# The FFN's hidden units: 128x128 transposes on TensorE through PSUM, or 32x32 block transposes on VectorE

## The chip, the core and the metric

The kernel runs on one core of one Trainium2 chip. The metric is the time of one execution on the device, in microseconds (us), as the median of several runs. The core's engines run side by side: TensorE (PE in the profile, with its weight loads as PEld), VectorE (DVE), ScalarE (ACT), GpSimd (POOL) and SyncE (SP), which here issues the loads of the weights.

## What is computed

The reference is one layer of a decoder trunk for 256 tokens of width 2048. First comes a token mixer, which the change doesn't touch, then a feed-forward network (FFN) with 5632 inner units:

```python
def channel_mixing(h, w_gate_up, w_down, g_pre, g_post):
    xn = rmsnorm(h, g_pre)
    gu = jnp.einsum('bld,df->blf', xn, w_gate_up)
    gate, up = gu[..., :FFN_HIDDEN], gu[..., FFN_HIDDEN:]
    y = jnp.einsum('blf,fd->bld', jax.nn.silu(gate) * up, w_down)
    return rmsnorm(y, g_post)
```

All of it is float32. The kernel keeps the precision by splitting each operand into a rounded part `hi` and a remainder `lo`, and by three matmuls for each product (hi·hi, hi·lo, lo·hi).

## The kernel before

**Splitting weights.** `load` (L84 to L88) brings 1 MB of weights into one of three `raw` buffers by a DMA from SP's queue. `split` (L90 to L98) makes two pairs `hi`, `lo` of 128x1024 elements from it: ScalarE casts `raw` into `hi` (L95), VectorE subtracts `hi` from `raw` into `lo` (L96). There are four `hi` and four `lo` buffers. So a cast waits until TensorE is through with the buffer four pairs earlier, the subtraction waits for the cast, TensorE waits for both, and the next load of a `raw` buffer waits for its last subtraction.

**Gate and up.** The loop over `gi` (L829) goes through 11 groups of 512 inner units. In each, `c` runs over four blocks of 512 input features and `s` over gate and up; for each of these 1 MB is loaded and split into two pairs (`gu_load`), and `gu_part` issues the matmuls L738, L739, L740: the stationary side is the normed input `x2hi` or `x2lo` (128 features x 128 tokens), the moving side 512 columns of weights. A pair takes 12 matmuls (two k, two token halves i, three products), a group 192. For c below 3 the pairs are used one after the other; for c = 3 each token half i is finished in turn, and `gu_evac` (L742) then takes the two banks out of PSUM: ScalarE's Silu writes `hg` (L745), VectorE multiplies by the up half (L746). `hg` has tokens on its partitions and 512 units in its rows, one tile for each half i, with four buffers in the pool `ft`. Even groups accumulate in the four PSUM banks `mx`, odd groups in the four `acc`.

**Turning.** The down product needs the units on the partitions. `hidden_out(gi, hgs, bank)` (L751) does that one group late, behind block c = 0 of the next group, so that TensorE doesn't wait for `hg`: for each half i, four TensorE transposes of 128x128 (L764, with `ident`) into a PSUM bank, then ScalarE's cast into `hidhi` (L767, 128x512) and VectorE's subtraction into `hidlo` (L768, 128x512). The last group's call stands in the down product, behind its first chunk (`after_first`, L646). Groups 0 to 3 of the units lie in tiles that reuse the mixer's place (`hid`), groups 4 to 10 in two tiles of the pool `hp` (`hid2`).

**Down.** `ktile_product` (L623) runs over the output's two halves and over 44 blocks k of 128 units, two k for each load of 1 MB and one `hi`, `lo` pair for each k. Here the hidden units are the stationary side and the weights the moving one: 12 matmuls for each k (two i, two j, three products; L628, L629, L630).

**Order.** The program is written in one order, and a scheduler of the framework puts each engine's instructions in a fixed sequence: of those whose inputs are there in its own model of the time, the one that stands first in the program goes first. Each engine then works through its sequence strictly in order, waiting on semaphores.

Of the kernel before, what the change touches and what calls it, by code (L numbers as in the profile page):

```python
# [10 lines left out]
F32 = mybir.dt.float32  # L11
F32R = mybir.dt.float32r
BF16 = mybir.dt.bfloat16
AF = mybir.ActivationFunctionType
ALU = mybir.AluOpType
# [3 lines left out]
P = 128  # L19
# [3 lines left out]
NT = 256  # L23
T = NMETA + NT
HID = 5632
NF = HID // P
# [11 lines left out]
def tile_hybrid_layer(  # L38
# [20 lines left out]
    vec, act, pe, pool, sp = nc.vector, nc.scalar, nc.tensor, nc.gpsimd, nc.sync  # L59
# [12 lines left out]
    def nm(s):  # L72
        uid[0] += 1
        return f"{s}_{uid[0]}"

    def acc(i):
        return psa.tile([P, 512], F32, tag=f"acc{i}", name=nm("acc"))

    def mx():
        return psm.tile([P, 512], F32, tag="mx", name=nm("mx"))  # L80
# [3 lines left out]
    def load(view, nk, w):  # L84
        raw = rawp.tile([P, 2 * MB], F32, tag="raw", name=nm("raw"), bufs=RAWB)
        r = raw[:, : nk * w].rearrange("p (k c) -> p k c", c=w)
        sp.dma_start(out=r, in_=view)
        return r  # L88
# [16 lines left out]
    ident = cst.tile([P, P], F32, name="ident")  # L105
# [29 lines left out]
    def win_view(k0, nk, c0, w):  # L135
        return w_in[0, k0 * P : (k0 + nk) * P, c0 : c0 + w].rearrange("(k p) c -> p k c", p=P)
# [402 lines left out]
    def first(kind, i):  # L539

        if kind in ("sbq", "o"):
            return NMETA
        if kind == "q":
            return NMETA - 4
        if kind == "pool":
            return NMETA - WINDOWS[i]
        return 0

    def load_group(ka, kb, blocks):
        nb = len(blocks)  # L550
        starts = [base[kind] + P * i for kind, i in blocks]
        raw = rawp.tile([P, 2 * MB], F32, tag="raw", name=nm("raw"), bufs=RAWB)
        r = raw[:, : (kb - ka) * nb * P].rearrange("p (k c) -> p k c", c=nb * P)
        j = 0
        while j < nb:
            e = j + 1
            while e < nb and starts[e] == starts[e - 1] + P:
                e += 1
            sp.dma_start(out=r[:, :, j * P : e * P], in_=win_view(ka, kb - ka, starts[j], (e - j) * P))
            j = e  # L560
        return r

    for gi, blocks in enumerate(groups):
        nb = len(blocks)
        w = P * nb
        accs = [acc(b) for b in range(nb)]
# [5 lines left out]
        for ka, kb in spans:  # L572
            if gi == 0:
# [5 lines left out]
                r = chunks[ka] if ka in chunks else load(win_view(ka, kb - ka, OG, 396), kb - ka, 396)  # L579
            else:  # L580
                r = load_group(ka, kb, blocks)
            subs = []
            for k0 in range(ka, kb, 2):
                rs = r[:, k0 - ka : k0 - ka + 2]
                if gi == 0:
                    gsrc = rs[:, :, 0:12].rearrange("p k (a b) -> p k a b", a=2)
                    dst = [gw[:, j, k0 : k0 + 2, :].rearrange("p k (a b) -> p k a b", a=2)[:, :, :, 0:6]
                           for j in range(2)]
                    for a in range(2):
                        act.copy(out=dst[0][:, :, a], in_=gsrc[:, :, a])  # L590
                        vec.tensor_tensor(out=dst[1][:, :, a], in0=gsrc[:, :, a], in1=dst[0][:, :, a].bitcast(F32),
                                          op=ALU.subtract)
                    rs = rs[:, :, 12:]
                subs.append((k0, split(rs, 2, w)))
            last = kb == KT
            passes = [subs] if last else [[s] for s in subs]
            for ss in passes:
                for b, (kind, i) in enumerate(blocks):
                    ts = slice(first(kind, i), T)
# [20 lines left out]

    mhi, mlo_ = mix_tiles()

    def ktile_product(wview, nk, half, accs, lhs, on_block, ticks=False, before_tail=None, after_first=None):  # L623

        def three(k, i, j, h, l):
            lh, ll = lhs(k, i)
            o, js = accs[i][j], slice(j * 512, (j + 1) * 512)
            pe.matmul(o, lhsT=lh, rhs=h[:, 0, js], start=k == 0, stop=False)  # L628
            pe.matmul(o, lhsT=lh, rhs=l[:, 0, js], start=False, stop=False)  # L629
            pe.matmul(o, lhsT=ll, rhs=h[:, 0, js], start=False, stop=k == nk - 1)  # L630

        pend = []
        for ci in range(0, nk, 2):
            r = load(wview(ci, half), 2, 1024)
            for kk in range(2):
                pend.append((ci + kk, split(r[:, kk : kk + 1], 1, 1024)))
            if ci + 4 < nk:
                for k, (h, l) in pend:
                    for i in range(2):
                        for j in range(2):  # L640
                            three(k, i, j, h, l)
                        if ticks:
                            tick()
                pend = []
            if ci == 0 and after_first:
                after_first()  # L646
        if before_tail:
            before_tail()
        for i in range(2):
            for j in range(2):  # L650
                for k, (h, l) in pend:
                    three(k, i, j, h, l)
                on_block(i, j)
# [36 lines left out]
    assert not queue and not active and not quick  # L690
    mixst.close()
    fp = ctx.enter_context(tc.tile_pool(name="fp", bufs=1))
    ft = ctx.enter_context(tc.tile_pool(name="ft", bufs=4, side="right"))
    exst = ExitStack()
    yp = exst.enter_context(tc.tile_pool(name="yp", bufs=1))
    ex = exst.enter_context(tc.tile_pool(name="ex", bufs=4))
# [42 lines left out]
                pe.matmul(o, lhsT=x2hi[:, k, ts], rhs=l[:, kk, :], start=False, stop=False)  # L739
                pe.matmul(o, lhsT=x2lo[:, k, ts], rhs=h[:, kk, :], start=False, stop=k == KT - 1)  # L740

    def gu_evac(banks, i):  # L742
        sc = rr[:, 1, i : i + 1]
        hg = ft.tile([P, 512], F32, tag="hg", name=nm("hg"))
        act.activation(hg, banks[0][i], AF.Silu, scale=sc)  # L745
        vec.scalar_tensor_tensor(out=hg, in0=banks[1][i], scalar=sc, in1=hg, op0=ALU.mult, op1=ALU.mult)  # L746
        return hg

    hidden = []

    def hidden_out(gi, hgs, bank):  # L751

        if gi < 8 and gi % 4 == 0:
            for s in ("hi", "lo"):
                if gi == 0:
                    q = big.tile([P, 16, NT], F32R, tag=f"mix{s}", name=f"hid{s}")
                    hidden.append([q[:, 4 * g : 4 * g + 4] for g in range(4)])
                else:
                    q = hp.tile([P, 28, NT], F32R, name=f"hid{s}2")
                    hidden[s == "lo"] += [q[:, 4 * g : 4 * g + 4] for g in range(7)]  # L760
        for i, hg in enumerate(hgs):
            pt = bank(i)
            for b in range(4):
                pe.transpose(pt[:, b * P : (b + 1) * P], hg[:, b * P : (b + 1) * P], ident)  # L764
            p4 = pt.rearrange("p (a b) -> p a b", b=P)
            ts = slice(i * P, (i + 1) * P)
            act.copy(out=hidden[0][gi][:, :, ts], in_=p4)  # L767
            vec.tensor_tensor(out=hidden[1][gi][:, :, ts], in0=p4, in1=hidden[0][gi][:, :, ts].bitcast(F32),  # L768
                              op=ALU.subtract)

    fg_split, later = {}, []
    fg_banks = []

    def four(gi):
        f = [mx() for _ in range(4)] if gi % 2 == 0 else [acc(b) for b in range(4)]
        return [f[0:2], f[2:4]]

    def spare(gi):
        return (lambda i: mx()) if gi % 2 == 0 else acc


    def fg_begin():
# [44 lines left out]
    hp = ctx.enter_context(tc.tile_pool(name="hp", bufs=1))  # L827

    for gi in range(11):  # L829
        banks = fg_banks if gi == 0 else four(gi)  # L830
        hgs = []
        for c in range(1 if gi == 0 else 0, 4):
            for s in range(2):
                subs = gu_load(c, gi, s)
                if c == 3:
                    for i in range(2):
                        gu_part(banks, s, i, subs)
                        if s == 1:
                            hgs.append(gu_evac(banks, i))
                else:  # L840
                    for sub in subs:
                        for i in range(2):
                            gu_part(banks, s, i, [sub])
            if c == 0:
                hidden_out(gi - 1, later, spare(gi - 1))
        later = hgs


    gpost2 = big.tile([P, KT * T], F32, tag="xlo", name="gfp")[:, :D]
# [8 lines left out]
    for half in range(2):  # L858
        flat = [acc(b) for b in range(4)] if half == 0 else [mx() for _ in range(4)]
        accs = [flat[0:2], flat[2:4]]  # L860

        def lhs_h(k, i):
            ts = slice(i * P, (i + 1) * P)
            return hidden[0][k // 4][:, k % 4, ts], hidden[1][k // 4][:, k % 4, ts]

        def done2(i, j, half=half, accs=accs):
            with tc.high_priority():
                finish_ffn(i, j, half, accs)

        def finish_ffn(i, j, half, accs):  # L870
            post_evac(accs, i, 2 * half + j, yg2, gpost2, ssz)
            if half == 0 or j == 0:
                return
            for c0, c1 in ((0, 640), (640, 1280), (1280, 1792), (1792, 2048)):
                cs = slice(c0, c1)
                vec.scalar_tensor_tensor(out=yg2[:, i, cs], in0=yg2[:, i, cs], scalar=rr[:, 0, i : i + 1],
                                         in1=h2[:, i, cs], op0=ALU.mult, op1=ALU.add)
                sp.dma_start(out=out_v[:, i, cs], in_=yg2[:, i, cs])

        last = (lambda: hidden_out(10, later, spare(10))) if half == 0 else None  # L880
        ktile_product(wd_view, NF, half, accs, lhs_h, done2, after_first=last)


# [27 lines left out]
```

## Time and profile before

| | |
|---|---|
| median of 3 runs | 1134.98 us (1134.49 to 1135.25) |
| the profiled execution | 1134.61 us, span of its trace 1132.9 us |
| busy, share of the span | PEld 85%, DVE 55%, ACT 44%, POOL 2% (PE: rows below) |
| DMA | 208.56 MB, mean 184 GB/s |
| VectorE's `lo` (L96), all shapes | x384, 459.7 us |
| ScalarE's `hi` (L95), all shapes | x384, 393.8 us |

A row of the timeline gives start, duration, engine, line, operation, the tile written and those read, the shapes, and in brackets how long the engine had been idle and what released it. Matmuls are pipelined: one shows some 0.39 us, but the next starts earlier, so that start to start is what one costs. The chain of waits is followed back from the last instruction of the program; each of its pieces is what the end waited for at that time.

### The profile page before, as it was taken

The page shows a single profiled execution, that of the slowest core. Times are in us where ns is not written, and L with a number is a line of the kernel's source. Part 1 is how long each engine was busy: PE and PEld are TensorE (multiplying, and loading weights), DVE is VectorE, ACT ScalarE, POOL GpSimd, SP SyncE. Part 2 cuts the span into 40 slices and gives each one's busy share as a digit, 9 for nine tenths or more (in the row PEclk, how much of TensorE's full clock was granted, in tenths as well). Part 3 has the DMA queues.
Part 4 walks back from the last instruction along what each step waited for, and adds up shares of the span by engine and source line. Part 5 has one row for each costly group of instructions (what it writes and reads, how often), then busy time and mean ns, then how long its engine had stood idle before and what let it go on. Part 6 is the DMA issues. An engine that isn't in the chain of part 4 may idle for free.

```text
span 1132.9 us, 14585 instructions
## 1 busy us (share of the span) xinstructions
PE 1121.4 (99%) x5951; PEld 964.8 (85%) x5951; DVE 626.5 (55%) x767; ACT 501.5 (44%) x671; POOL 22.8 (2%) x66
## 2 busy tenths in 40 slices
PE   9999999999999999999999999999999999999997
PEld 7999999999988788888888888888888888888885
DVE  4777755759945865445454454454454444454444
ACT  6544455534434754444444444444444433343332
POOL 4000000000000000000000000000000000000000
PEclk9999999999999999999999999999999999999999
DMA  7654643544485556555555555555555655556551
GB/s 242 187 179 144 199 150 112 176 140 149 150 333 186 186 169 202 180 193 186 186 186 190 188 188 196 196 194 185 186 186 186 225 191 189 190 193 200 186 186 74
DMA packets 100546, 208.56 MB, mean 184 GB/s; under 512 B 3962, under 2 KB 31402, under 8 KB 99952
## 3 DMA queue, kind: packets, MB, share of 16 engines
q1 hardware_dynamic: 99168, 201.58, 54.5%
q0 software_dynamic: 896, 2.92, 0.9%
q10 hardware_dynamic: 416, 3.15, 0.7%
q8 instruction: 46, 0.75, 0.3%
q14 instruction: 20, 0.16, 0.0%
HBM read 205.52 MB, written 2.11 MB: 183 GB/s over the span
## 4 chain that ended last, share of the span: by engine, by line
PE 98%; DVE 1%; DMA 0%; ACT 0%; issue 0%; SPq 0%; DVEq 0%; POOLq 0%; ACTq 0%
PE mx L738 8%; PE mx L740 8%; PE mx L739 8%; PE acc L102 7%; PE acc L100 7%; PE acc L101 7%; PE acc L739 6%; PE acc L740 6%; PE acc L738 6%; PE mx L629 5%; PE acc L629 5%; PE mx L630 5%; PE mx L628 5%; PE acc L630 5%; PE acc L628 5%; PE mx L764 0%
## 5 line engine op out<-in xcount | busy, mean ns | idle before, releaser
L96 DVE TENSOR_TENSOR lo<-raw,hi 128x1024 fp32r<-128x1024 f32 (+1 forms) x384 | 459.7, 1201 | 445.2 <-ACT hi L95 443.5
L95 ACT CAST hi<-raw 128x1024 fp32r<-128x1024 f32 (+1 forms) x384 | 393.8, 1029 | 516.6 <-PE mx L740 132.5
L102 PE MATMUL acc<-xhi,lo 128*128 128x272 f32 (+4 forms) x640 | 192.0, 300 | 0.0
L100 PE MATMUL acc<-xhi,hi 128*128 128x272 f32 (+4 forms) x640 | 187.1, 292 | 0.4 <-DVE im L294 0.4
L101 PE MATMUL acc<-xlo,hi 128*128 128x272 f32 (+4 forms) x640 | 186.5, 291 | 0.0
L738 PE MATMUL mx<-hi,x2hi 128*128 128x512 f32 x384 | 150.1, 391 | 0.0
L740 PE MATMUL mx<-hi,x2lo 128*128 128x512 f32 x384 | 149.7, 390 | 0.0
L739 PE MATMUL mx<-lo,x2hi 128*128 128x512 f32 x384 | 149.5, 389 | 0.0
L738 PE MATMUL acc<-hi,x2hi 128*128 128x512 f32 x320 | 124.9, 390 | 0.0
L740 PE MATMUL acc<-hi,x2lo 128*128 128x512 f32 x320 | 124.6, 389 | 0.0
L739 PE MATMUL acc<-lo,x2hi 128*128 128x512 f32 x320 | 124.5, 389 | 0.0
L100 PEld LDWEIGHTS acc<-xhi,hi 128*128 128x128 f32 x640 | 121.5, 190 | 2.2 <-issue 1.4
L102 PEld LDWEIGHTS acc<-xhi,lo 128*128 128x128 f32 x640 | 121.3, 190 | 1.6 <-issue 1.0
L101 PEld LDWEIGHTS acc<-xlo,hi 128*128 128x128 f32 x640 | 121.3, 190 | 0.3
L740 PEld LDWEIGHTS mx<-hi,x2lo 128*128 128x128 f32 x384 | 72.1, 188 | 15.0
L738 PEld LDWEIGHTS mx<-hi,x2hi 128*128 128x128 f32 x384 | 72.1, 188 | 14.9 <-ACT x2hi L821 0.2
L739 PEld LDWEIGHTS mx<-lo,x2hi 128*128 128x128 f32 x384 | 72.1, 188 | 14.7
L740 PEld LDWEIGHTS acc<-hi,x2lo 128*128 128x128 f32 x320 | 60.1, 188 | 12.5
L738 PEld LDWEIGHTS acc<-hi,x2hi 128*128 128x128 f32 x320 | 60.1, 188 | 12.3
L739 PEld LDWEIGHTS acc<-lo,x2hi 128*128 128x128 f32 x320 | 60.1, 188 | 12.3
L629 PE MATMUL mx<-lo,hidhi 128*128 128x512 f32 x176 | 69.4, 394 | 0.0
L629 PE MATMUL acc<-lo,hidhi 128*128 128x512 f32 x176 | 69.2, 393 | 0.0
(230 smaller groups left out, 1208.9 us busy)
## 6 DMA issues: line engine op xcount, KB each, us to landing
raw<-in_w_gate_up_dram SPq DMA_DIRECT2D x88, 1024.0 KB, 5.1
raw<-in_w_down_dram SPq DMA_DIRECT2D x44, 1024.0 KB, 5.1
raw<-in_w_in_dram SPq DMA_DIRECT2D x36, 512.0 KB, 4.7
raw<-in_w_out_dram SPq DMA_DIRECT2D x16, 1024.0 KB, 5.2
raw<-in_w_in_dram SPq DMA_DIRECT2D x12, 1024.0 KB, 5.1
raw<-in_w_in_dram SPq DMA_DIRECT2D x8, 768.0 KB, 4.5
raw<-in_w_in_dram SPq DMA_DIRECT2D x3, 792.0 KB, 7.0
h<-in_x_dram ACTq DMA_DIRECT2D x1, 2048.0 KB, 12.1
```

Source lines behind the costliest of these rows:

```text
L95: act.copy(out=h, in_=r)
L96: vec.tensor_tensor(out=l, in0=r, in1=h.bitcast(F32), op=ALU.subtract)
L100: pe.matmul(o, lhsT=wh, rhs=xh, start=start, stop=False, **kw)
L101: pe.matmul(o, lhsT=wh, rhs=xl, start=False, stop=False, **kw)
L102: pe.matmul(o, lhsT=wl, rhs=xh, start=False, stop=stop, **kw)
L628: pe.matmul(o, lhsT=lh, rhs=h[:, 0, js], start=k == 0, stop=False)
L629: pe.matmul(o, lhsT=lh, rhs=l[:, 0, js], start=False, stop=False)
L630: pe.matmul(o, lhsT=ll, rhs=h[:, 0, js], start=False, stop=k == nk - 1)
L738: pe.matmul(o, lhsT=x2hi[:, k, ts], rhs=h[:, kk, :], start=k == 0, stop=False)
L739: pe.matmul(o, lhsT=x2hi[:, k, ts], rhs=l[:, kk, :], start=False, stop=False)
L740: pe.matmul(o, lhsT=x2lo[:, k, ts], rhs=h[:, kk, :], start=False, stop=k == KT - 1)
```

## The change

Eight transposes of a group on TensorE are replaced by sixteen VectorE instructions, each on 32 partitions. `hg` becomes one tile for both token halves (128 x 2 x 512). A new tile `ht` (128 x 4 x 256, in the pool `hp`, one buffer) takes the units with tokens in the rows. For each quarter j of `ht`'s partitions and each quarter a of `hg`'s, one `vec.transpose` reads 32 partitions x 256 elements of `hg`, transposes every 32x32 block, and writes 32 partitions x 256 elements of `ht`. Then ScalarE casts `ht` into `hidhi` and VectorE subtracts, each in one instruction of 128x1024 from SBUF, where it was two of 128x512 from PSUM. `hidden_out` becomes a generator in three steps: transposes for j = 0, 1; transposes for j = 2, 3; cast and subtraction. `next(later, None)` takes one step behind each block c of the following group, and for the last group behind each chunk of the down product. No PSUM bank is needed for the turning.

```diff
-    def ktile_product(wview, nk, half, accs, lhs, on_block, ticks=False, before_tail=None, after_first=None):
+    def ktile_product(wview, nk, half, accs, lhs, on_block, ticks=False, before_tail=None, after=None):
...
-            if ci == 0 and after_first:
-                after_first()
+            if after:
+                after()
...
-    ft = ctx.enter_context(tc.tile_pool(name="ft", bufs=4, side="right"))
+    ft = ctx.enter_context(tc.tile_pool(name="ft", bufs=1, side="right"))
...
-    def gu_evac(banks, i):
+    def gu_evac(banks, i, hg):
         sc = rr[:, 1, i : i + 1]
-        hg = ft.tile([P, 512], F32, tag="hg", name=nm("hg"))
-        act.activation(hg, banks[0][i], AF.Silu, scale=sc)
-        vec.scalar_tensor_tensor(out=hg, in0=banks[1][i], scalar=sc, in1=hg, op0=ALU.mult, op1=ALU.mult)
-        return hg
+        g = hg[:, i, :]
+        act.activation(g, banks[0][i], AF.Silu, scale=sc)
+        vec.scalar_tensor_tensor(out=g, in0=banks[1][i], scalar=sc, in1=g, op0=ALU.mult, op1=ALU.mult)
...
-    def hidden_out(gi, hgs, bank):
+    def hidden_out(gi, hg):
...
-        for i, hg in enumerate(hgs):
-            pt = bank(i)
-            for b in range(4):
-                pe.transpose(pt[:, b * P : (b + 1) * P], hg[:, b * P : (b + 1) * P], ident)
-            p4 = pt.rearrange("p (a b) -> p a b", b=P)
-            ts = slice(i * P, (i + 1) * P)
-            act.copy(out=hidden[0][gi][:, :, ts], in_=p4)
-            vec.tensor_tensor(out=hidden[1][gi][:, :, ts], in0=p4, in1=hidden[0][gi][:, :, ts].bitcast(F32),
-                              op=ALU.subtract)
-
-    fg_split, later = {}, []
+        ht = hp.tile([P, 4, NT], F32, tag="ht", name=nm("ht"))
+        src = hg.rearrange("p i (b j s) -> p i b j s", j=4, s=32)
+        dst = ht.rearrange("p b (i a r) -> p i b a r", i=2, r=32)
+        for j in range(4):
+            for a in range(4):
+                vec.transpose(out=dst[32 * j : 32 * j + 32, :, :, a, :], in_=src[32 * a : 32 * a + 32, :, :, j, :])
+            if j % 2:
+                yield
+        act.copy(out=hidden[0][gi], in_=ht)
+        vec.tensor_tensor(out=hidden[1][gi], in0=ht, in1=hidden[0][gi].bitcast(F32), op=ALU.subtract)
+        yield
+
+    fg_split, later = {}, iter(())
...
-        hgs = []
+        hg = ft.tile([P, 2, 512], F32, tag="hg", name=nm("hg"))
...
-                            hgs.append(gu_evac(banks, i))
+                            gu_evac(banks, i, hg)
...
-            if c == 0:
-                hidden_out(gi - 1, later, spare(gi - 1))
-        later = hgs
+            next(later, None)
+        later = hidden_out(gi, hg)
...
-        last = (lambda: hidden_out(10, later, spare(10))) if half == 0 else None
-        ktile_product(wd_view, NF, half, accs, lhs_h, done2, after_first=last)
+        ktile_product(wd_view, NF, half, accs, lhs_h, done2, after=lambda: next(later, None))
```

## Rows read from the trace of the kernel before

**Rows 1.** The page: span, busy time, and the chain that ended last by engine.
```profile
span 1132.9 us, 14585 instructions
...
PE 1121.4 (99%) x5951; PEld 964.8 (85%) x5951; DVE 626.5 (55%) x767; ACT 501.5 (44%) x671; POOL 22.8 (2%) x66
...
PE 98%; DVE 1%; DMA 0%; ACT 0%; issue 0%; SPq 0%; DVEq 0%; POOLq 0%; ACTq 0%
```

**Rows 2.** Busy time by stretch: PE, PEld, DVE, ACT, POOL, granted clock, DMA share, GB/s.
```profile
490.50:535.00 44.50, 44.50 (x202) 36.92 (x201) 22.07 (x21) 19.00 (x20) 0.00 (x0) 1.00 0.58 191
```

**Rows 3.** Chain of waits: start, duration, piece; first, second and last of eleven like them.
```profile
446.48 0.87 PE mx L764 x8
490.90 0.87 PE acc L764 x8
...
885.30 0.87 PE mx L764 x8
```

**Rows 4.** Timeline of PE around the transposes of one group.
```profile
490.51 0.39 PE L740 MATMUL mx<-hi,x2lo 128*128 128x512 f32 x1
490.74 1.03 PE L764 MATMUL acc<-ident,hg 128*128 128x128 f32 x8
491.53 0.48 PE L738 MATMUL mx<-hi,x2hi 128*128 128x512 f32 x1
491.85 0.39 PE L739 MATMUL mx<-lo,x2hi 128*128 128x512 f32 x1
```

**Rows 5.** The instructions of line L764: duration in ns (min/median/max), first and last start.
```profile
L764 PE MATMUL mx<-ident,hg x48: 270/272/273, 446.3 to 885.9; 128*128 128x128 f32 x48
```

**Rows 6.** Groups of instructions on DVE by line and shape: busy us, mean ns, idle before.
```profile
L96 DVE TENSOR_TENSOR lo<-raw,hi 128x1024 fp32r<-128x1024 f32 x352 | 429.4, 1224 | 427.5 <-ACT hi L95 427.3
...
L409 DVE RECIPROCAL slot<-slot 128x256 f32<-128x256 f32 x6 | 10.5, 1749 | 0.1
...
L768 DVE TENSOR_TENSOR hidlo<-mx,hidhi 128x512 fp32r<-128x512 f32 x12 | 7.7, 682 | 0.0
...
L394 DVE SCALAR_TENSOR_TENSOR slot<-slot,ucol,mlm 128x256 f32<-128x256 f32 x6 | 2.8, 474 | 2.6 <-DMA slot<-M_d 2.6
...
L412 DVE TENSOR_TENSOR slot<-slot,sig 128x256 f32<-128x256 f32 x6 | 2.5, 419 | 0.0
```

**Rows 7.** Timeline of DVE: two stretches, in group 2 and behind group 10.
```profile
481.58 1.22 DVE L96 TENSOR_TENSOR lo<-raw,hi 128x1024 fp32r<-128x1024 f32 x1
483.86 1.23 DVE L96 TENSOR_TENSOR lo<-raw,hi 128x1024 fp32r<-128x1024 f32 x1 [1.06 <-ACT hi L95]
...
492.02 1.23 DVE L96 TENSOR_TENSOR lo<-raw,hi 128x1024 fp32r<-128x1024 f32 x1 [1.50 <-ACT hi L95]
493.17 1.28 DVE L768 TENSOR_TENSOR hidlo<-acc,hidhi 128x512 fp32r<-128x512 f32 x2
...
880.76 0.74 DVE L746 SCALAR_TENSOR_TENSOR hg<-mx,rr,hg 128x512 f32<-128x512 f32 x1
881.42 1.22 DVE L96 TENSOR_TENSOR lo<-raw,hi 128x1024 fp32r<-128x1024 f32 x1
883.70 1.23 DVE L96 TENSOR_TENSOR lo<-raw,hi 128x1024 fp32r<-128x1024 f32 x1 [1.06 <-ACT hi L95]
```

**Rows 8.** Waits of SP's DMA queue from 446 to 880 us: total, times, longest.
```profile
SPq L87 <- DVE lo L96: 398.8, 78, 5.9
```

**Rows 9.** Timeline of PE in the down product: its start, and around block k = 16.
```profile
879.70 0.39 PE L628 MATMUL acc<-hi,hidhi 128*128 128x512 f32 x1
...
920.95 0.39 PE L629 MATMUL acc<-lo,hidhi 128*128 128x512 f32 x1
...
923.67 0.39 PE L629 MATMUL acc<-lo,hidhi 128*128 128x512 f32 x1
```

**Rows 10.** Chain of waits in the down product: two pieces, 12 matmuls apart.
```profile
930.13 0.24 PE acc L629
932.93 0.24 PE acc L629
```

More of the change, by code (lines that the diff above doesn't have):

```diff
@@ L776, in four @@
         return [f[0:2], f[2:4]]
-    def spare(gi):
-        return (lambda i: mx()) if gi % 2 == 0 else acc
     def fg_begin():
```

## The prediction

> **What bounds the kernel now.** I read the page first, and in it the chain that ended last: TensorE makes up 98% of it and is busy in 99% of the span [rows 1]. So TensorE is the bound, and other engines matter only where they would make it wait. Next I took the busy time by stretch, one group of the gate and up product at a time: TensorE is busy in all 44.50 us at granted clock 1.00, while VectorE works 22.07 us, ScalarE 19.00, and the DMA engines have a share of 0.58 [rows 2]. The chain of waits then says whether the transposes to be removed lie on the path: eleven pieces of eight transposes stand in it, 0.87 us each, and the first two start 44.42 us apart, which is the period of a group [rows 3]. Last, the timelines of TensorE and VectorE around one such piece tell what it costs and where VectorE has room.
>
> **The part removed: 88 transposes on TensorE.** A transpose shows a duration of 272 ns [rows 5], but these overlap. What counts is how far the matmuls behind them are pushed back. In group 2 the last matmul ahead starts at 490.51, the second behind at 491.85, 1.34 us later [rows 4]. Without the transposes they would be two spacings apart. One spacing comes from a stretch without transposes, with matmuls of the same shape: 12 of them take 2.72 us (920.95 to 923.67) [rows 9], or 0.227 us each. So the eight cost 1.34 - 0.45 = 0.89 us, close to the chain's 0.87. Eleven groups: 11 x 0.89 = 9.8 us, all of it on the path, because TensorE never waits beside them. I take 9.8, with 9.6 (11 x 0.87) as the other end.
>
> [...]
>
> **The part added: 176 block transposes on VectorE.** No transpose runs on VectorE before, so its price t (32 partitions x 256 elements, float32) must be bounded. The nearest rows have 256 elements in a row: 0.419 us for a plain two-input operation, 0.474 with a scalar pointer; the longest operation of that size is the reciprocal with 1.749 [rows 6]. A transpose only moves its elements, once each, which puts it nearest to the first two; I take 0.45, and keep 0.42 and 1.75 as ends.
>
> [...]
>
> *Where they hide.* VectorE's queue is in order, so the question is which `lo` stands behind them. The step for j = 0, 1 stands behind block c = 0. In group 2 the last `lo` of that block ends at 481.58 + 1.22 = 482.80, and the product that makes `hg` is already done [rows 7]. Eight transposes then take 482.80 to 486.40. The `lo` behind them ran at 483.86 before [rows 7]; it would now end at 486.40 + 1.23 = 487.63. TensorE needs it for the second matmul of block c = 1, which without transposes ahead starts at 490.51 + 2 x 0.227 = 490.96 [rows 4]. So 3.3 us are left of the 5.9 that this `lo` has now (it ends at 485.09), and the place breaks even at t = (490.96 - 482.80 - 1.23)/8 = 0.87. The second eight stand behind block c = 1, or run in VectorE's idle gaps of some 1.5 us ahead of each `lo` [rows 7]; the slack is alike.
>
> *Load.* Per group VectorE loses two subtractions of 0.682, gains one of 128x1024 at about 1.224 [rows 6] and sixteen transposes: 22.07 - 1.36 + 1.22 + 16 x 0.45 = 29.1 us in a period of 44.42 - 0.89 = 43.5. It has room up to t = (43.5 - 21.9)/16 = 1.35; order fails before load does.
>
> *Who else waits.* A late `lo` also delays the load of a `raw` buffer: SP's queue waits for `lo` all the time, 78 times and 398.8 us in total [rows 8], which says that loads come far ahead of their use and are held back by buffers alone; with the DMA share at 0.58, a delay of 3.6 us is covered. ScalarE's cast of `ht` waits for the sixteenth transpose, and the casts behind it in ScalarE's queue wait too; behind them come `lo` with the same 5.9 us in hand, so I cost this at nothing. If the cast stood so early in the queue that it waited longer than that, the cover would go. One cast of 128x1024 for two of 128x512 moves ScalarE by a tenth of a us. `hg` with one buffer costs nothing: its last reader comes behind block c = 1, the next Silu only in block c = 3. No DMA is added or moved.
>
> *Group 10.* Its two steps fall into the down product, where a chunk has only two pairs (5.44 us) and not four. `hg` is there at 880.76 + 0.74 = 881.50 [rows 7]. If eight transposes go ahead of the `lo` at 881.42 and eight behind it, the `lo` that ran at 883.70 [rows 7] ends at 881.50 + 3.60 + 1.22 + 3.60 + 1.23 = 891.15. It is for k = 4, first needed at 879.70 + 48 x 0.227 + 0.23 = 890.8 [rows 9]. That is 0.35 us late, once; 0.42 makes it nothing, 0.474 makes it 0.7. I take 0.3.
>
> **Sum.** 9.8 - 0.3 = 9.5 us off the profiled execution's 1134.61 (its span is 1132.9): 1125.1. The median of the runs is 0.37 above that execution, so 1125.5 on the median.
>
> **Rivals.**
>
> *Slower: the block transposes are long, and TensorE waits for `lo` twice a group.* This decides at t = 0.87, and the two waits 2 x 8 x (t - 0.87) outgrow the 0.89 saved at t = 0.93. At t = 1.0 a group is 2.1 - 0.9 = 1.2 us longer, ten groups 12 us, and group 10 gives 16 + 2.45 - 9.3 = 9 us: about 1155. At the reciprocal's 1.75 VectorE itself is the bound, 21.9 + 28 = 49.9 us for a group, 5.5 more than 44.42: 55 us in ten groups and some 18 in the down product, about 1208. For it: the instruction reads and writes in runs of 32 elements and crosses partition quarters, which no row shows. Against it: it would have to take twice what other instructions of this length take. Chance 0.08.
>
> *No change that can be told:* t near 0.9, so that what TensorE saves it spends waiting, or another limit takes the 0.89 us. Nothing points to one: DMA and ScalarE have room [rows 2]. About 1134. Chance 0.04.
>
> *The spacing of the down product moves.* From k = 16 on, 12 matmuls take 2.80 us (930.13 to 932.93) [rows 10], before that 2.72 [rows 9]. The step comes where the stationary side changes from `hid` to `hid2`; the two tiles differ in their place in SBUF, and the trace doesn't show why that costs. The new `ht` stands in the same pool and shifts `hid2` by 4 KB. If the 2.80 became 2.72, 28 k in two halves would give back 56 x 0.08 = 4.5 us: 1121.0; if the step doubled, 1130.0. Chance 0.08, more for nothing at all, which is in the forecast.
>
> *The change frees more than the trace shows*, a full 272 ns for each transpose [rows 5]: 88 x 0.272 = 24 us, 1111. The start times of the matmuls speak against it. Chance 0.01. [...]
>
> **How the numbers follow.** The forecast as worked out has 0.79. A measurement of this kernel can tell about 0.2%, or 2.3 us, from no change. Faster than that are the forecast, both cases of the spacing and the last rival: 0.79 + 0.08 + 0.01 = 0.88. Same 0.04, slower 0.08. The range goes from 1121.0 to 1130.0: it holds the forecast with both ends of its costs (9.6 to 10, 0 to 0.7), the cases of the spacing, and transposes late by up to 0.4 us a group; left out are the other three rivals, 0.13.
>
> **What would show it.** Right: no L764 in the chain; groups 43.5 us apart; the new transposes at 0.42 to 0.48 us; TensorE without a gap at the change from block c = 0 to c = 1; VectorE at some 29 us in a group; a gap of under a us, if any, near k = 4 of the down product. Wrong: transposes over 0.87 us, or VectorE's `lo` in the chain in each group; TensorE waiting behind a ScalarE cast held by `ht`; a spacing of matmuls other than 2.72 and 2.80 per 12.

## The result, and the profile after

The changed kernel takes 1125.23 us (median of 4 runs, 1124.69 to 1125.51) against 1135.01 before (1134.49 to 1135.25): a ratio of 0.9914, 95% interval 0.9902 to 0.9927. The forecast was 1125.5. The profiled execution took 1125.51 us, with a span of 1123.6.

The page of the kernel after, with the answers to [rows 1]: busy time, the chain by engine, and the new group of transposes.

```profile
span 1123.6 us, 14563 instructions
...
PE 1112.4 (99%) x5863; PEld 956.3 (85%) x5863; DVE 700.2 (62%) x932; ACT 501.3 (45%) x660; POOL 22.8 (2%) x66
...
PE 97%; DVE 2%; DMA 1%; ACT 0%; issue 0%; SPq 0%; DVEq 0%; POOLq 0%; ACTq 0%
...
L766 DVE STREAM_TRANSPOSE ht<-hg 32x256 f32<-32x256 f32 x176 | 76.7, 436 | 2.8
```

TensorE has 88 matmuls less (5951 to 5863) and is still the bound. VectorE works 74 us more, in 176 transposes of 436 ns. Two per cent of the chain now lie on VectorE, where it was one: from 869 to 884 us, the place behind group 10 below, some 11 us of the chain run through its instructions.

Busy time by stretch, kernel after, columns as in [rows 2], the same 44.50 us:

```profile
490.50:535.00 44.50, 44.50 (x198) 36.84 (x198) 29.76 (x36) 19.82 (x20) 0.00 (x0) 1.00 0.60 198
```

VectorE's 22.07 us have become 29.76. TensorE has no gap, which the timeline of PE shows in detail (kernel after: start of group 2, the change from its block c = 0 to c = 1, the start of group 3):

```profile
479.20 0.39 PE L738 MATMUL mx<-hi,x2hi 128*128 128x512 f32 x1
...
489.86 0.39 PE L740 MATMUL mx<-hi,x2lo 128*128 128x512 f32 x1
490.08 0.39 PE L738 MATMUL mx<-hi,x2hi 128*128 128x512 f32 x1
490.31 0.39 PE L739 MATMUL mx<-lo,x2hi 128*128 128x512 f32 x1
...
522.72 0.39 PE L738 MATMUL acc<-hi,x2hi 128*128 128x512 f32 x1
```

Where eight transposes stood in [rows 4], the matmuls now follow each other at 0.22 to 0.23 us. A group takes 522.72 - 479.20 = 43.52 us, 0.9 less than the 44.42 of [rows 3]; read from the start times, all matmuls from 410 to 881 us come at 2.72 us for 12.

What VectorE does meanwhile (timeline of DVE, kernel after, group 2, to be held against [rows 7]):

```profile
480.93 1.21 DVE L96 TENSOR_TENSOR lo<-raw,hi 128x1024 fp32r<-128x1024 f32 x1
482.06 3.57 DVE L766 STREAM_TRANSPOSE ht<-hg 32x256 f32<-32x256 f32 x8
485.66 1.23 DVE L96 TENSOR_TENSOR lo<-raw,hi 128x1024 fp32r<-128x1024 f32 x1
486.92 0.43 DVE L766 STREAM_TRANSPOSE ht<-hg 32x256 f32<-32x256 f32 x1
487.38 1.23 DVE L96 TENSOR_TENSOR lo<-raw,hi 128x1024 fp32r<-128x1024 f32 x1
488.64 1.79 DVE L766 STREAM_TRANSPOSE ht<-hg 32x256 f32<-32x256 f32 x4
```

Eight in a row behind the last `lo` of block c = 0, then a `lo` that ends at 486.89 and is needed by the L739 at 490.31: 3.4 us in hand, where 3.3 were worked out. The second eight are spread over the gaps between the following `lo`.

Behind group 10 it is otherwise. Timeline of DVE, kernel after, start of the down product:

```profile
872.61 1.21 DVE L96 TENSOR_TENSOR lo<-raw,hi 128x1024 fp32r<-128x1024 f32 x1
873.74 7.17 DVE L766 STREAM_TRANSPOSE ht<-hg 32x256 f32<-32x256 f32 x16
880.95 2.36 DVE L96 TENSOR_TENSOR lo<-raw,hi 128x1024 fp32r<-128x1024 f32 x2
```

And the timeline of PE there:

```profile
881.53 0.39 PE L630 MATMUL acc<-hi,hidlo 128*128 128x512 f32 x1
881.76 0.39 PE L628 MATMUL acc<-hi,hidhi 128*128 128x512 f32 x1
882.23 0.50 PE L629 MATMUL acc<-lo,hidhi 128*128 128x512 f32 x1
882.57 0.40 PE L630 MATMUL acc<-hi,hidlo 128*128 128x512 f32 x1
```

All sixteen stand in one row ahead of the `lo` for k = 4, whose first user (L629) starts at 882.23 and not at 881.99; the matmul behind it follows after 0.34 us and not 0.23. That is 0.24 + 0.11 us; by the start times the 24 matmuls around it take 3.09 + 2.77 us in place of 2 x 2.72, 0.42 us in all.

### The profile page after: what moved, and what is told of

Same layout as the page of the kernel before. It is cut to its first block, busy times and chain, and to the rows that moved or that the text cites. A ratio compares the mean times of both kernels' runs of the same rounds, so it can differ in the third digit from the quotient of the medians.

```text
span 1123.6 us, 14563 instructions
## 1 busy us (share of the span) xinstructions
PE 1112.4 (99%) x5863; PEld 956.3 (85%) x5863; DVE 700.2 (62%) x932; ACT 501.3 (45%) x660; POOL 22.8 (2%) x66
## 4 chain that ended last, share of the span: by engine, by line
PE 97%; DVE 2%; DMA 1%; ACT 0%; issue 0%; SPq 0%; DVEq 0%; POOLq 0%; ACTq 0%
PE mx L738 8%; PE mx L740 8%; PE mx L739 8%; PE acc L102 7%; PE acc L100 7%; PE acc L101 7%; PE acc L738 6%; PE acc L739 6%; PE acc L740 6%; PE mx L629 5%; PE mx L628 5%; PE mx L630 5%; PE acc L629 5%; PE acc L630 5%; PE acc L628 5%; DVE ht L766 1%
## 5 line engine op out<-in xcount | busy, mean ns | idle before, releaser
L738 PE MATMUL mx<-hi,x2hi 128*128 128x512 f32 x384 | 149.7, 390 | 0.0
L739 PE MATMUL mx<-lo,x2hi 128*128 128x512 f32 x384 | 149.6, 389 | 0.0
L738 PE MATMUL acc<-hi,x2hi 128*128 128x512 f32 x320 | 124.6, 389 | 0.0
L739 PE MATMUL acc<-lo,x2hi 128*128 128x512 f32 x320 | 124.5, 389 | 0.0
L740 PEld LDWEIGHTS mx<-hi,x2lo 128*128 128x128 f32 x384 | 72.1, 188 | 15.1
L738 PEld LDWEIGHTS mx<-hi,x2hi 128*128 128x128 f32 x384 | 72.1, 188 | 15.0 <-ACT x2hi L820 0.2
L739 PEld LDWEIGHTS mx<-lo,x2hi 128*128 128x128 f32 x384 | 72.1, 188 | 14.8
L766 DVE STREAM_TRANSPOSE ht<-hg 32x256 f32<-32x256 f32 x176 | 76.7, 436 | 2.8
L738 PEld LDWEIGHTS acc<-hi,x2hi 128*128 128x128 f32 x320 | 60.1, 188 | 12.4
L739 PEld LDWEIGHTS acc<-lo,x2hi 128*128 128x128 f32 x320 | 60.1, 188 | 12.4
L629 PE MATMUL acc<-lo,hidhi 128*128 128x512 f32 x176 | 69.4, 394 | 0.1
```

The source lines that it names most:

```text
L738: pe.matmul(o, lhsT=x2hi[:, k, ts], rhs=h[:, kk, :], start=k == 0, stop=False)
L766: vec.transpose(out=dst[32 * j : 32 * j + 32, :, :, a, :], in_=src[32 * a : 32 * a + 32, :, :, j, :])
```

## The experiments

Medians are compared with the changed kernel's 1125.23 us; where a ratio stands, it is to the kernel before, timed beside the run.

**1. No transposes at all.** The cast and the subtraction read `hg` in the order in which it lies; the block transposes are left out.

```diff
-        for j in range(4):
-            for a in range(4):
-                vec.transpose(out=dst[32 * j : 32 * j + 32, :, :, a, :], in_=src[32 * a : 32 * a + 32, :, :, j, :])
-            if j % 2:
-                yield
-        act.copy(out=hidden[0][gi], in_=ht)
-        vec.tensor_tensor(out=hidden[1][gi], in0=ht, in1=hidden[0][gi].bitcast(F32), op=ALU.subtract)
+        yield
+        yield
+        hv = hg.rearrange("p i (b u) -> p b i u", b=4)
+        o0 = hidden[0][gi].rearrange("p b (i u) -> p b i u", i=2)
+        o1 = hidden[1][gi].rearrange("p b (i u) -> p b i u", i=2)
+        act.copy(out=o0, in_=hv)
+        vec.tensor_tensor(out=o1, in0=hv, in1=o0.bitcast(F32), op=ALU.subtract)
```

> Left out: the sixteen block transposes of each group; the cast and the subtraction read hg directly, so the down product works on wrongly ordered units. Theory (the transposes are hidden but for the wait behind group 10): every group stays at 2.72 us for 12 matmuls, the pieces of 3.09 and 2.77 us per 12 near k = 4 of the down product go back to 2.72, and the time falls by about 0.4 us, to 1124.8 us. Rival (the transposes also cost TensorE something, by contention for SBUF or by waits too small to see): the time falls by 1 us or more, to 1124 us or less.

Measured: 1124.93 us (1124.33 to 1125.40), ratio 0.9914 (0.9897 to 0.9930). The timeline of PE of this kernel, around k = 4 of the down product, has no gap:

```profile
881.47 0.39 PE L628 MATMUL acc<-hi,hidhi 128*128 128x512 f32 x1
881.69 0.39 PE L629 MATMUL acc<-lo,hidhi 128*128 128x512 f32 x1
881.92 0.39 PE L630 MATMUL acc<-hi,hidlo 128*128 128x512 f32 x1
```

Its start times give 2.72 us for 12 all the way from 410 us to k = 15. The 77 us of transposes on VectorE cost the kernel 0.3 us by the medians (within their scatter) and 0.4 by the trace. The rival, 1 us or more, falls.

**2. Every transpose twice**, sixteen to a step.

```diff
-            for a in range(4):
+            for a in [q for q in range(4) for _ in range(2)]:
```

> Each block transpose is issued twice, so that a step has sixteen of 0.436 us in place of eight. Theory (what decides is how many stand ahead of one lo in VectorE's order, with room for 8 x 0.87 us): 16 x 0.45 = 7.2 us ahead of a lo that has room for 6.9, so TensorE waits 0.2 to 1.3 us in each group and about 7 us in all behind group 10: 1134 to 1146 us, with VectorE's lo in the chain. Rival (only VectorE's load counts, 21.9 + 32 x 0.45 = 36.3 us of 43.5 in a group): no wait in the groups, 1125 us, or 1132 with the wait behind group 10.

Measured: 1152.5 us, ratio 1.0156 (1.0136 to 1.0176): slower than the kernel before. Timeline of DVE of this kernel, group 2:

```profile
484.33 7.31 DVE L766 STREAM_TRANSPOSE ht<-hg 32x256 f32<-32x256 f32 x16
491.67 3.50 DVE L96 TENSOR_TENSOR lo<-raw,hi 128x1024 fp32r<-128x1024 f32 x3
...
497.39 6.43 DVE L766 STREAM_TRANSPOSE ht<-hg 32x256 f32<-32x256 f32 x14
```

Timeline of PE of this kernel at the same places:

```profile
492.36 0.39 PE L738 MATMUL mx<-hi,x2hi 128*128 128x512 f32 x1
492.95 0.50 PE L739 MATMUL mx<-lo,x2hi 128*128 128x512 f32 x1 [0.21 <-DVE lo L96]
493.29 0.39 PE L740 MATMUL mx<-hi,x2lo 128*128 128x512 f32 x1
...
505.13 0.50 PE L739 MATMUL mx<-lo,x2hi 128*128 128x512 f32 x1 [1.00 <-DVE lo L96]
```

Its waits, 405 to 1100 us (total, times, longest):

```profile
PEld acc L739 <- DVE lo L96: 10.3, 10, 1.4
PEld mx L739 <- DVE lo L96: 10.3, 10, 1.4
...
PE acc L629 <- DVE lo L96: 6.9, 1, 6.9
```

TensorE waits for `lo` twenty times in ten groups and once long behind group 10, though VectorE has some 10 us of each group to spare (it works 349.76 of the 450 us from 440 to 890). The rival (load alone) falls. The size was above my range: by the start times 12 matmuls take 3.09 and 2.85 us around the first wait, 3.90 and 2.85 around the second, against 2.72. That is 1.8 us for a group, where 0.2 to 1.3 were expected: the two `lo` are 0.36 and some 1.17 us late together with their first matmul, and behind each wait come another 0.13, most of it the matmul at 493.29, which follows after 0.34 us and not 0.23.

The second wait is the longer one, though only fourteen of the second sixteen transposes stand in one row ahead of its `lo`. VectorE hadn't caught up by then: the fourteen start at 497.39, the matmul was due at 503.98 and its `lo` takes 1.23, so the room was 5.4 us and not 6.9. The expectation had given both steps the full room.

Behind group 10 about 7 us were expected. The matmul there comes 7.05 us late, but by the start times the place costs 9.5 us against none, because matmuls behind the wait were slower too: those of L629 and L630 into `acc` have a mean of 401 and 400 ns here, 394 and 393 in the changed kernel. Run 5 shows such a place in rows. Ten times 1.8 and 9.5, less the 0.4 that the changed kernel loses there itself, make 27.1 us; 27.3 were measured.

**3. TensorE's transposes put back**, into PSUM banks that nobody reads, beside the block transposes.

```diff
+        if gi % 2 == 0:
+            pts = [mx(), mx()]
+        else:
+            pts = [acc(0), acc(1)]
+        for i in range(2):
+            for b in range(4):
+                pe.transpose(pts[i][:, b * P : (b + 1) * P], hg[:, i, b * P : (b + 1) * P], ident)
         for j in range(4):
```

> The changed kernel, with the eight TensorE transposes of each group put back ahead of the block transposes; they write PSUM banks that nobody reads. Theory (the whole gain is TensorE's 0.89 us for eight transposes in each of eleven groups): the time goes up by 9.8 us, to 1135.0 us, and the matmuls around the eight are pushed back by 0.89 us. Rival (part of the gain comes from elsewhere, from VectorE and ScalarE no longer reading these PSUM banks or from the merged cast and subtraction): less than 9 us are lost, 1130 to 1134 us.

Measured: 1135.32 us (1134.43 to 1135.65), ratio 1.0005 (0.9996 to 1.0014): the whole gain is gone. Timeline of PE of this kernel, group 2:

```profile
491.09 0.39 PE L740 MATMUL mx<-hi,x2lo 128*128 128x512 f32 x1
491.32 1.04 PE L770 MATMUL acc<-ident,hg 128*128 128x128 f32 x8
...
492.42 0.39 PE L739 MATMUL mx<-lo,x2hi 128*128 128x512 f32 x1
```

From the matmul ahead to the second behind it are 1.33 us, two spacings and 0.88. By the start times, from the first L738 to the last L630, this kernel takes 734.9 us and the changed kernel 725.4. The 9.5 us between them are about eleven times 0.89 less the 0.4 of the wait at k = 4, which this kernel doesn't have: with TensorE pushed back, that `lo` comes in time. The kernel before takes 734.9 us for the same stretch. So nothing else of the change (the merged cast and subtraction, PSUM banks left alone) is worth a measurable amount.

**4. `hid2` moved on by 32 bytes.** The prediction left open why 12 matmuls take 2.80 us from k = 16 on. No trace shows addresses. In those that the framework gave the tiles, the two sides of a matmul with `hid2` leave different remainders by 64. The two sides of the other matmuls with 512 columns agree, but for the first 48 of gate and up, whose weights lie in buffers of their own. Some small matmuls of the mixer don't agree either, so "all the other operands", as the expectation has it, is too wide.

```diff
+    fp.tile([P, 8], F32, name="pad")
     hp = ctx.enter_context(tc.tile_pool(name="hp", bufs=1))
```

> A pad of 32 bytes ahead of the pool hp moves ht and both hid2 tiles on by 32 bytes, so that their addresses leave the same remainder by 64 as those of all the other operands of the matmuls (32, where hid2 had 0). Theory A (the spacing depends on whether the stationary and the moving side agree in that remainder): 12 matmuls take 2.72 us and not 2.80 from k = 16 on, the time falls by 4.5 us to 1120.7 us. Rival (the place in SBUF as such, or the tile's size, or the units' groups 4 to 10 cost it): still 2.80 us, 1125.2 us.

Measured: 1121.0 us (1120.67 to 1121.57), ratio 0.9879 (0.9864 to 0.9894), 4.2 us less than the changed kernel. Timeline of PE, the changed kernel, two matmuls 12 apart beyond k = 16 (2.80 us):

```profile
929.76 0.39 PE L629 MATMUL acc<-lo,hidhi 128*128 128x512 f32 x1
...
932.56 0.39 PE L629 MATMUL acc<-lo,hidhi 128*128 128x512 f32 x1
```

The same of the moved kernel (2.72 us):

```profile
930.08 0.39 PE L629 MATMUL acc<-lo,hidhi 128*128 128x512 f32 x1
...
932.80 0.39 PE L629 MATMUL acc<-lo,hidhi 128*128 128x512 f32 x1
```

**5. Half as many transposes more**, twelve to a step, between the eight that are hidden and the sixteen that are not.

```diff
-            for a in range(4):
+            for a in (0, 0, 1, 1, 2, 3):
```

> Four of the eight block transposes of a step are issued twice, so that a step has twelve. Theory (order decides, with room for 6.9 us ahead of a lo): 12 x 0.45 = 5.4 us fit, so TensorE waits nowhere in the ten groups (2.72 us for every 12 matmuls), and only behind group 10, where 24 x 0.45 = 10.8 us stand ahead of the lo for k = 4: it would come 3.7 us late, 1128.9 us. Rival (what a transpose costs rises evenly from eight to sixteen, the 27 us of the doubled kernel halved): waits in each group, about 1139 us.

Measured: 1129.4 us (1129.35 and 1129.45). The only row of this kernel's waits on PE, 405 to 1100 us:

```profile
PE acc L629 <- DVE lo L96: 3.1, 1, 3.1
```

The groups keep 2.72 us for 12 matmuls throughout, and the loss stands in one place behind group 10. Costs don't rise evenly from eight to sixteen: there is a threshold between 5.4 and 7.2 us in front of one `lo`, as worked out (6.9).

Timeline of PE behind group 10, and busy time of the stretch behind the wait (columns as in [rows 2]):

```profile
885.55 0.50 PE L629 MATMUL acc<-lo,hidhi 128*128 128x512 f32 x1 [3.14 <-DVE lo L96]
...
887.77 0.63 PE L630 MATMUL acc<-hi,hidlo 128*128 128x512 f32 x1
888.20 0.63 PE L628 MATMUL acc<-hi,hidhi 128*128 128x512 f32 x1
```

```profile
886.50:890.00 3.50, 3.50 (x11) 2.68 (x10) 3.50 (x5) 1.04 (x1) 0.00 (x0) 0.53 0.56 178
```

The matmul for k = 4 comes 3.3 us late, where 3.7 were expected. Then something follows that no forecast had: behind the wait TensorE's granted clock is 0.53 on the mean of 3.5 us, and eight matmuls come 0.43 us apart and not 0.23; the last piece of 0.43 in the chain starts at 889.68. By the start times the place costs 5.0 us against none, 3.3 of it lateness and some 1.6 the clock. That 1129.4 lies so near the expected 1128.9 is therefore partly luck: the expectation left the clock out, had the lateness too long, and counted the changed kernel's own 0.4 us at this place twice.

**6. Every operand moved on by 32 bytes**, which keeps gate and up agreed and leaves `hid2` apart from the weights.

```diff
     cst = ctx.enter_context(tc.tile_pool(name="cst", bufs=1))
+    cst.tile([P, 8], F32, name="pad")
```

> A pad of 32 bytes at the start of the first pool moves every operand of the matmuls on by 32 bytes: weights, x2 and hid then have remainder 0 by 64, hid2 has 32. Theory A (it counts whether the two sides of a matmul agree): nothing changes, 2.72 us for 12 matmuls up to k = 15, 2.80 from k = 16, 1125.2 us. Rival B (a stationary side at remainder 0 is slow by itself): 2.80 us in all of gate and up and up to k = 15, 2.72 from k = 16: about 1125.2 + 16 + 1 = 1142 us. Rival C (a moving side at remainder 0 is better): gate and up below 2.72 us.

Measured: 1125.06 us (1124.92 and 1125.21), no change. Timeline of PE of this kernel, in gate and up (2.72 us for 12) and beyond k = 16 (2.80); its lines are one further on:

```profile
430.19 0.39 PE L740 MATMUL mx<-lo,x2hi 128*128 128x512 f32 x1
...
432.91 0.39 PE L740 MATMUL mx<-lo,x2hi 128*128 128x512 f32 x1
...
930.15 0.40 PE L630 MATMUL acc<-lo,hidhi 128*128 128x512 f32 x1
...
932.95 0.40 PE L630 MATMUL acc<-lo,hidhi 128*128 128x512 f32 x1
```

Here `hid2` has the remainder that gave 2.72 us in run 4, and 12 matmuls take 2.80. So it is the two sides' agreement, not the address of one.

**7. The kernel before with the pad of run 4**, and nothing else.

> The kernel before, with the 32 bytes of pad ahead of the pool hp and nothing else. Theory (the spacing has nothing to do with the change): 12 matmuls take 2.72 us from k = 16 on here too, 1134.6 - 4.2 = 1130.4 us. Rival (it takes the new layout of the pool hp as well): no change, 1134.6 us.

Measured: 1130.26 us (1129.89 to 1130.62), ratio 0.9957 (0.9942 to 0.9972), 4.4 us less than its own 1134.66. The spacing is a matter apart from the change.

**8. The changed kernel with the pad, and the last group in four steps.**

```diff
+    fp.tile([P, 8], F32, name="pad")
...
-            if j % 2:
+            if j % 2 or gi == 10:
                 yield
```

> The changed kernel with the 32 bytes of pad ahead of hp, and with the last group's sixteen block transposes taken in four steps of four, one behind each of the down product's first four chunks. Theory: the wait near k = 4 goes (the piece of 3.09 us per 12 matmuls goes back to 2.72) and with it 0.4 us, the spacing gives 4.2: 1120.6 us. Rival (the wait moves to a later lo): 1121.0 us.

Measured: 1120.85 us (1120.36 to 1121.06), ratio 0.9873 (0.9856 to 0.9889), the fastest of all. Timeline of DVE of this kernel, start of the down product:

```profile
873.87 3.57 DVE L766 STREAM_TRANSPOSE ht<-hg 32x256 f32<-32x256 f32 x8
877.47 1.23 DVE L96 TENSOR_TENSOR lo<-raw,hi 128x1024 fp32r<-128x1024 f32 x1
```

The `lo` for k = 4 now runs after eight transposes, and the start times show 2.72 us for 12 from 410 to 982 us without a break. Against run 4 the median gains 0.15 us, less than the two runs' scatter: that the wait is gone is shown by the trace, its worth of 0.4 us isn't shown by the times.

**9. The weights against everything else by 32 bytes**: a pad between their buffers and all pools behind them.

```diff
+    pd = ctx.enter_context(tc.tile_pool(name="pd", bufs=1))
+    pd.tile([P, 8], F32, name="pad3")
     big = ctx.enter_context(tc.tile_pool(name="big", bufs=1))
```

> A pad of 32 bytes between the weights' buffers and all pools behind them: the weights keep remainder 32 by 64, x2, hid and the mixer's output get 0, hid2 gets 32. Theory A (the two sides of a matmul must agree): 12 matmuls take 2.80 us in gate and up (176 times 12, 14.1 us), in the output product of the mixer and up to k = 15 of the down product (32 times each, 2.6 us each), and 2.72 from k = 16 (4.2 us less): 1140 us, and more if the mixer's input product with 272 columns is touched as well. Rival (only the tiles in hid2's place or of its size are slow when at remainder 0): 1121 us.

Measured: 1138.85 us (median of six; five lie between 1138.32 and 1139.24, one took 5402 us for a reason that wasn't looked into). Timeline of PE of this kernel, gate and up (2.80 us for 12) and beyond k = 16 (2.72); its lines are two further on:

```profile
430.06 0.40 PE L740 MATMUL mx<-hi,x2hi 128*128 128x512 f32 x1
...
432.86 0.40 PE L740 MATMUL mx<-hi,x2hi 128*128 128x512 f32 x1
...
949.84 0.39 PE L631 MATMUL acc<-lo,hidhi 128*128 128x512 f32 x1
...
952.56 0.39 PE L631 MATMUL acc<-lo,hidhi 128*128 128x512 f32 x1
```

Fast and slow stretches have changed places, and the mixer's output product takes 2.80 too. The terms add up to 14.1 + 2.6 + 2.6 - 4.2 = 15.1 us and 13.6 were measured. By the start times gate and up take 13.7 us more than in the changed kernel, the mixer's output product 1.9 more, and the down product 2.1 less, of which 0.4 is the wait at k = 4 that this kernel no longer shows.

One product shows no such difference. In the mixer's input product, where the weights are the stationary side, the pad parts the two sides as well; yet its matmuls with 272 columns come 0.125 us apart here and 0.126 in the changed kernel (medians of the start times). So the effect is shown for 512 columns with the weights as the moving side, and for nothing else.

## Why the prediction was right, point by point

- *The part removed.* 0.89 us for eight transposes, eleven times, 9.8 us, all on the path. Run 3 puts just that back and gets the old time. The duration of 272 ns for each [rows 5] would have given 24 us; the pushback in the timeline was the right reading.
- *The price of a block transpose.* 0.45 was taken between rows of 0.419 and 0.474, by likeness alone; 0.436 was measured, 0.45 from start to start. That it fits so closely is partly luck, but little hung on it, since the groups had room up to 0.87. Crossing partition quarters and runs of 32 elements, the arguments for the slower rival, cost nothing that shows.
- *Where they hide.* Run 1 shows that the transposes cost nothing but the wait behind group 10. Runs 5 and 2 bracket the threshold for the first step of a group: twelve (5.4 us) fit in front of a `lo`, sixteen (7.2) don't, and 6.9 was worked out as 8 x 0.87. So the rival of long transposes has the right mechanism and the right place, and only its condition wasn't met. What the sum of that rival missed is the price beyond the threshold: in run 2 a group lost 1.8 us, where its formula, with twice the transposes for twice t, 2 x 8 x (0.90 - 0.87), gave 0.5. It took the two steps of a group as independent, but VectorE enters the second one late from the first.
- *Load.* 29.1 us for VectorE in a group were expected; 29.76 stand in the same 44.50 us as before, which is 0.98 us longer than a group now is.
- *Who else waits.* ScalarE's cast of `ht` does wait for the transposes, as said, 1.76 us in group 2 of the changed kernel, and nothing behind it comes late. The row, from the timeline of ACT:

```profile
493.10 1.05 ACT L769 CAST hidhi<-ht 128x1024 fp32r<-128x1024 f32 x1 [1.76 <-DVE ht L766]
```

- *Group 10.* 0.35 us late was worked out and 0.3 taken; 0.24 late was measured, and 0.42 us of cost. The order was not quite the one supposed (sixteen behind one `lo`, not eight ahead and eight behind), but the same instructions stand ahead of the `lo` for k = 4. That 0.3 lies between the two is luck: the sum took the lateness for the cost and had no term for the slower matmul behind the wait.
- *The sum.* In the chain, from the first matmul behind the last transposes of L817 (L816 after) to ScalarE's L672 behind the last matmul, the time fell from 1125.06 - 400.84 = 724.2 to 1115.77 - 401.09 = 714.7 us, by the 9.5 of the sum. Ahead of that stretch, where both kernels have the same instructions, the second one ran 0.25 us later.
- *The spacing.* The forecast held it at 2.80 with `ht` ahead of `hid2`, and so it stayed: 4 KB doesn't change the remainder. That rival's chance of 0.08 was for want of its cause, which runs 4, 6, 7 and 9 gave.

## What to carry to other kernels

Cost an instruction on a full engine by how far it pushes back the next one, not by its duration; here the two differ by a factor of two and a half. Work that moved to an engine with room was free here as long as what stood in one piece ahead of a needed instruction in that engine's queue was shorter than the slack of that instruction (5.4 us of transposes against 6.9 in run 5); beyond it the price jumped (1.8 us for a group in run 2, with 7.2 us), and behind the waits of 3 and 7 us in runs 5 and 2 matmuls were slower too (0.43 us apart in run 5). So split such work into steps, and look above all at stretches where the steps come closer together. And compare the start addresses of a matmul's two sides: here a pad of 32 bytes was worth 4.2 us (run 4), nearly half of the 9.8 us of this change.

## What the runs showed of the hardware that was not expected

- *Start addresses.* 12 float32r matmuls of 128x128 by 128x512 took 2.72 us in some stretches and 2.80 in others (0.227 and 0.233 us each), at granted clock 1.00 in both (changed kernel, 441 to 485 and 921 to 1005 us). Moving the two sides by 32 bytes against each other turned the one into the other: 2.80 into 2.72 with `hid2` moved (runs 4 and 7), 2.72 into 2.80 in gate and up with the weights apart from the rest (run 9). With both sides moved on together each stretch kept its time (run 6). The matmuls with 272 columns and stationary weights in run 9 show no such difference (0.125 us, 0.126 in the changed kernel). The remainders by 64 are read from the framework's addresses; no other distance than 32 bytes was tried, so whether 64 is the modulus isn't shown.
- *A wait of TensorE costs more than the lateness.* Behind the short waits shown, in the changed kernel (882.23 to 882.57) and in run 2's groups (492.95 to 493.29), the next matmul followed after 0.34 us and not 0.23. The weight load stood in the open there: in run 2 that of the L739 at 492.95 starts together with it, where the next ones, at 493.06 and 493.29, start 0.23 us ahead of theirs. That this is the cause fits the rows and wasn't tried. Timeline of PEld of run 2:

```profile
492.95 0.19 PEld L739 LDWEIGHTS mx<-lo,x2hi 128*128 128x128 f32 x1 [0.63 <-DVE lo L96]
```

- *The clock fell behind a long wait.* Behind run 5's idle time of 3.14 us the granted clock was 0.53 from 886.5 to 890 us, where the changed kernel has 1.00 from 402 to 1110 us, and 512-column matmuls came 0.43 us apart. The first matmuls behind the wait still came faster: in the chain the wait ends at 885.55, the first slower piece starts at 886.75 and the last at 889.68. Behind run 2's idle time of 6.9 us the place cost 9.5 us, 2.4 more than its lateness; no row gives its clock. Behind run 2's idle times of 0.21 and 1.00 us in the groups the matmuls came 0.23 us apart again from the second on (493.29 to 493.52, 505.47 to 505.70).
- *Block transposes don't overlap.* Eight took 3.57 us, 0.448 each from start to start with 0.436 of duration, while a `lo` starts before the one ahead ends (three in 3.50 us, 1.224 each). No run shows the cause.
